# Stick-breaking attention scores: the keys' low part of two heads in one page, each head's product over 64 rows of the array

## The chip, the cores and the metric

The kernel runs on one core of one Trainium2 chip. The metric is device time in microseconds (us) of one execution. Before the change it is 1696.86 us, the median of three runs (1694.31 to 1698.92).

## The reference, cut to what matters

The layer normalises its input, runs three token mixers on it (stick-breaking attention, mLSTM, cross-attention), merges them and ends with a gated MLP. The change touches the scores of the first mixer, 8 heads of 64 dimensions over 1024 positions:

```
z = jnp.einsum('bhtd,bhsd->bhts', q[:, :, t0:t1], k[:, :, :t1]).astype(jnp.float32) * scale
strict = jnp.arange(t1)[None, :] < (t0 + q_pos)[:, None]
log_fail = jnp.where(strict, jax.nn.log_sigmoid(-z), 0.0)
log_after = lax.cumsum(log_fail, axis=3, reverse=True) - log_fail
w = jnp.where(strict, jnp.exp(jax.nn.log_sigmoid(z) + log_after), 0.0)
outs.append(jnp.einsum('bhts,bhsd->bhtd', w.astype(v.dtype), v[:, :, :t1]))
```

## The kernel before, in words

**Precision.** TensorE multiplies numbers of a reduced form (`fp32r` in the rows). For nearly fp32 results the kernel splits operands: hi is the rounded value, lo is the rest, and a product is hi·hi + hi·lo + lo·hi. The large projections write this as three matmuls of 512 columns (`mm3`, lines 149 to 151).

**Scores of two heads.** The heads are taken in four pairs p = 0 to 3. The projected queries of a pair fill 128 partitions, 64 per head. `sb_qk` (line 364) lays them out so that one matmul over 128 rows does two of the three products: page `qs[a]` of head a holds the query's hi in the head's own 64 partitions and its lo in the other 64; page `ks[a]` holds the key's hi in both halves. So `qs[a]·ks[a]` is hi·hi + lo·hi. The third product, the query's hi with the key's lo, uses a page `kz[a]` per head: the key's lo in the head's own 64 partitions and zeros in the other 64, written once per pair by two memsets of GpSimd (POOL).

**Pieces.** Scores are made in pieces: one block of 128 queries (`rb`) against up to 4 blocks of 128 keys, so a matmul has 128 to 512 columns. Each pair of heads has 12 pieces. For a piece `sb_weights` (line 404) issues for head 0 the 128-row product (line 410), on pieces with the diagonal block the mask (line 412), and the product with `kz` (line 413); then the same for head 1. The PSUM tile `z` has one bank per head, and there is a single such tile. ScalarE (ACT) makes two sigmoids of it (`f` and `g`, lines 415 and 416), VectorE (DVE) a running product and a multiply (422, 424).

**What stands around a piece.** The loop over pieces issues, in this order: the scores of piece n; on two pieces of three half a unit of the next pair's projection (lines 149 to 151; for p = 3 the mLSTM values); the weighted sum of an earlier piece (`sb_apply`, line 448, matmuls whose weights are 64 columns wide, head 0 to PSUM partitions 0 to 63 and head 1 to 64 to 127); the transposes of the piece before (`sb_turn`, line 434), copied out of PSUM by ACT (line 436, tile `y`). Line 448 waits for that copy. Each engine works its instructions in a fixed order, found by a scheduler at build time with priorities; pages come from a ring of 16 buffers (`pg`), so a page less shifts which buffer a later page gets.

Of the kernel before, what the change touches and what calls it, by code (L numbers as in the profile page):

```python
# [10 lines left out]
F32 = mybir.dt.float32  # L11
F32R = mybir.dt.float32r
# [26 lines left out]
T_SBQ, T_SBK, T_MLQ, T_MLK, T_MLO, T_XAQ, T_GATE = 0, 4, 8, 12, 16, 20, 24  # L39
# [3 lines left out]
def tile_hybrid_layer(ctx: ExitStack, tc: tile.TileContext, xT, memT, vecs, w_t, w_n, w_kv, w_if,  # L43
# [4 lines left out]
    nc = tc.nc  # L48
# [19 lines left out]
    def T(shape, tag, dt=F32, bufs=None):  # L68
        pool = {"mw": mlp, "mst": mlp, "ga": mlp, "gm": mlp,  "px": late[0]}.get(tag, sb)
        return pool.tile(shape, dt, tag=tag, name=nm(tag), bufs=bufs or BUFS[tag])  # L70

    def page(tag="pg", dt=F32):
        return T([P, S], tag, dt)
# [7 lines left out]
    def two(tag):  # L81
        return psx[0].tile([P, 2, HALF], F32, tag=tag, name=nm("ps_" + tag), bufs=1)
# [6 lines left out]
    def bank(tag):  # L89
        if tag in ("pj", "pv"):  # L90
            return ps.tile([P, HALF], F32, tag=tag, name=nm("ps_" + tag), bufs=2)
        if px1 is not None:
            if not spare.get(tag):
                t = two(tag)
                spare[tag] = [t[:, 1], t[:, 0]]
            return spare[tag].pop()
        return psx[0].tile([P, HALF], F32, tag=tag, name=nm("ps_" + tag), bufs=2)
# [4 lines left out]
    def hs(h):  # L102
        return slice(h * HALF, (h + 1) * HALF)

    def ts(t):
        return slice(t * P, (t + 1) * P)
# [32 lines left out]
    def wsplit(src, tag=None, eng=None, raw=None):  # L139
        if raw is None:  # L140
            raw = T([P, S], "raw")
            nc.sync.dma_start(raw, src)
        hi = T([P, S], tag or "whi", F32R)
        lo = T([P, S], tag or "wlo", F32R)
        split(raw, hi, lo, eng)
        return hi, lo

    def mm3(out, lh, ll, rh, rl, start, stop, more=False):
        nc.tensor.matmul(out, lh, rh, start=start, stop=False, skip_group_check=more)  # L149
        nc.tensor.matmul(out, lh, rl, start=False, stop=False, skip_group_check=more)  # L150
        nc.tensor.matmul(out, ll, rh, start=False, stop=stop, skip_group_check=more)  # L151
# [8 lines left out]
    def rstd(acc, n):  # L160

        nt = n // P
        pc = bank("tr")
        for t in range(nt):
            nc.tensor.matmul(pc[:, t:t + 1], acc[:, ts(t)], ones[:, :1], start=True, stop=True)
        return rstd_cols(pc[:, :nt], nt, D)
# [103 lines left out]
    def x_stats(xp):  # L270
        acc = []
        for i in range(4):
            sq = wide()
            nc.scalar.activation(sq, xp[i], AF.Square)
            acc.append(sq)
            if i:
                nc.vector.tensor_add(acc[0], acc[0], sq)
        a = acc[0][:, hs(0)]
        nc.vector.tensor_add(a, a, acc[0][:, hs(1)])
        return a  # L280
# [37 lines left out]
    r = rstd(x_stats(xp[1]), HALF)  # L318
# [16 lines left out]
    def proj_chunks(src, consume, halves=(1, 0)):  # L335

        with tc.high_priority(offset=SOON):
            wh, wl = wsplit(src)
        for h in halves:
            p = bank("pj")  # L340
            for k in range(KT):
                mm3(p, wh[:, ts(k)], wl[:, ts(k)], hh[k][:, hs(h)], hl[k][:, hs(h)], k == 0, k == KT - 1)
                if k == 3:
                    yield
            consume(h, p)
            yield
# [17 lines left out]
    def sb_qk(p):  # L364
        qs = [page(dt=F32R) for _ in range(2)]
        ks = [page(dt=F32R) for _ in range(2)]
        kz = [page(dt=F32R) for _ in range(2)]
        A, B = slice(0, 64), slice(64, 128)
        nc.gpsimd.memset(kz[0][B].bitcast(F32), 0.0)
        nc.gpsimd.memset(kz[1][A].bitcast(F32), 0.0)  # L370

        def eq(h, b):
            c = hs(h)
            nc.scalar.activation(qs[0][A, c], b[A], AF.Copy)
            nc.scalar.activation(qs[1][B, c], b[B], AF.Copy)
            nc.vector.tensor_sub(qs[0][B, c], b[A], qs[0][A, c].bitcast(F32))
            nc.vector.tensor_sub(qs[1][A, c], b[B], qs[1][B, c].bitcast(F32))

        def ek(h, b):
            c = hs(h)  # L380
            nc.scalar.activation(ks[0][A, c], b[A], AF.Copy)
            nc.scalar.activation(ks[1][B, c], b[B], AF.Copy)
            nc.scalar.activation(ks[0][B, c], b[A], AF.Copy)
            nc.scalar.activation(ks[1][A, c], b[B], AF.Copy)
            nc.vector.tensor_sub(kz[0][A, c], b[A], ks[0][A, c].bitcast(F32))
            nc.vector.tensor_sub(kz[1][B, c], b[B], ks[1][B, c].bitcast(F32))

        return (qs, ks, kz), lambda *a: itertools.chain(proj_chunks(w_t[T_SBQ + p], eq, *a),
                                                        proj_chunks(w_t[T_SBK + p], ek, *a))

    y_d = [dtile([4, P, S], f"y{b}_d") for b in range(3)]
# [10 lines left out]
    acc_pv = [None]  # L402

    def sb_weights(p, st, rb, o):
        qs, ks, kz = st
        w = min(4, NCH - rb - o) * P
        c = slice((rb + o) * P, (rb + o) * P + w)
        z = two("z")
        for a in range(2):
            nc.tensor.matmul(z[:, a, :w], qs[a][:, ts(rb)], ks[a][:, c], start=True, stop=False)  # L410
            if o == 0:
                nc.tensor.matmul(z[:, a, :P], ident_r, mask_r, start=False, stop=False, skip_group_check=True)
            nc.tensor.matmul(z[:, a, :w], qs[a][:, ts(rb)], kz[a][:, c], start=False, stop=True)
        f, g = T([P, 2, HALF + 1], "U"), T([P, 2, HALF], "U")
        nc.scalar.activation(f[:, :, 1:w + 1], z[:, :, :w], AF.Sigmoid, scale=-0.125)  # L415
        nc.scalar.activation(g[:, :, :w], z[:, :, :w], AF.Sigmoid, scale=0.125)
        if o == 0:
            nc.gpsimd.memset(f[:, :, 0:1], 1.0)
        else:
            nc.vector.tensor_copy(f[:, :, 0:1], carry[0])  # L420
        for a in range(2):
            nc.vector.tensor_tensor_scan(f[:, a, 1:w + 1], f[:, a, 1:w + 1], f[:, a, 1:w + 1],  # L422
                                         1.0 if o == 0 else f[:, a, 0:1], op0=ALU.mult, op1=ALU.bypass)
        nc.vector.tensor_mul(g[:, :, :w], g[:, :, :w], f[:, :, 0:w])
        carry[0] = f[:, :, w:w + 1]
        return g
# [31 lines left out]
    def gates_if():  # L458
        for h in (1, 0):
# [10 lines left out]
            yield  # L470

    st, chunks = sb_qk(0)
    early = []
    for b in range(2):
# [18 lines left out]
    a = x_stats(xp[0])  # L493
    for _ in range(1):
        next(vals)
    r = rstd(a, HALF)
# [115 lines left out]
    for p in range(4):  # L612
        now = st
        if p < 3:
            st, chunks = sb_qk(p + 1)
            chunks = chunks()
        else:
            chunks = nat_chunks(1, ev_v, [0, 1, 2, 3, 7, 6, 5, 4])
        for n, (rb, o) in enumerate(PIECES):
            g = sb_weights(p, now, rb, o)  # L620
            if n % 3 < 2:
                next(chunks, None)
            if (p, n) == (0, 2):
                next(rows_step)
            apply_next()
            turn_next()
            weights.append((p, rb, o, g))
        if p < 3:
            for _ in chunks:
                pass  # L630
# [401 lines left out]
    for i in range(3 * KT):  # L1032
        b, n = i // KT, i % KT
# [5 lines left out]
        for h in (1, 0):  # L1039
            p = bank("pj")  # L1040
            for j in range(4):
                c = slice(((n % 2) * 4 + j) * P, ((n % 2) * 4 + j + 1) * P)
# [362 lines left out]
```

## Time and profile before

| | |
|---|---|
| median of the runs shown | 1696.86 us |
| profiled execution | 1701.33 us |
| its span, first to last instruction | 1699.6 us |
| PE (TensorE matmul) busy | 1664.2 us, 98% |
| PEld (weight loads, beside PE) | 1337.9 us, 79% |
| DVE, ACT, POOL busy | 1196.2, 823.8, 71.5 us |
| score stage, about 115 to 327 us | 212 us of the span |

The busy times come from one profiled execution. A matmul's recorded duration is longer than the time until the next one can start, since matmuls are pipelined: the cost of one in a row of them is read from start to start. An idle time in square brackets is counted from the recorded end of the matmul before.

### The profile page before, as it was taken

The numbers are of one execution on the slowest core, as the hardware profiler recorded it, in microseconds if no ns is written. First come the engines' busy times: TensorE is split into PE (matmuls) and PEld (weight loads), VectorE is DVE, ScalarE is ACT, GpSimd is POOL, SyncE is SP. The second block draws the span as 40 slices with busy tenths as digits, with TensorE's granted clock in tenths as the row PEclk, the third lists the DMA queues.
The fourth block names the chain that finished last, engine by engine and source line by source line (L and its number), as shares of the span: only waits on it lengthen the run. The fifth ranks groups of instructions, "written<-read, shape, count | busy, mean of one in ns | idle before, by whom it ended". The sixth has DMA issues, their size and how long they took to land.

```text
span 1699.6 us, 21431 instructions
## 1 busy us (share of the span) xinstructions
PE 1664.2 (98%) x7927; PEld 1337.9 (79%) x7927; DVE 1196.2 (70%) x1752; ACT 823.8 (48%) x1293; POOL 71.5 (4%) x149
## 2 busy tenths in 40 slices
PE   8999999999999999999999999999999999999999
PEld 4777777787777887777788888688888888788887
DVE  5648777677944665555457747998877787789864
ACT  4547677545544444555412334465555555543531
POOL 1000000020000221100000000000000000000000
PEclk9999999999999999999999999999999999999999
DMA  8321011233324555432666255132232222486042
GB/s 295 143 64 32 26 39 50 95 119 129 113 99 138 164 182 170 152 99 98 236 194 197 86 194 199 44 130 75 79 105 77 75 75 75 152 330 235 25 143 75
DMA packets 99069, 212.73 MB, mean 125 GB/s; under 512 B 13184, under 2 KB 41088, under 8 KB 98964
## 3 DMA queue, kind: packets, MB, share of 16 engines
q1 hardware_dynamic: 98964, 211.35, 36.7%
q8 instruction: 63, 1.03, 0.3%
q14 instruction: 42, 0.34, 0.1%
HBM read 156.71 MB, written 54.61 MB: 124 GB/s over the span
## 4 chain that ended last, share of the span: by engine, by line
PE 86%; ACT 4%; DVE 4%; DMA 3%; issue 2%; SPq 1%; POOL 0%; POOLq 0%; ACTq 0%; DVEq 0%
PE ps_pj L149 14%; PE ps_pj L150 13%; PE ps_pj L151 13%; PE ps_pv L150 6%; PE ps_pv L151 6%; PE ps_pv L149 6%; PE ps_tr L149 4%; PE ps_tr L150 4%; PE ps_tr L151 4%; PE ps_z L151 2%; PE ps_z L150 2%; PE ps_z L149 2%; PE ps_pv L448 2%; PE ps_tr L434 2%; DMA y<-qk_d 1%
## 5 line engine op out<-in xcount | busy, mean ns | idle before, releaser
L150 PE MATMUL ps_pj<-h,whi 128*128 128x512 f32 x620 | 244.1, 394 | 0.0
L136 ACT ACTIVATE whi<-raw 128x512 fp32r<-128x512 f32 (+1 forms) x112 | 93.6, 835 | 185.4 <-PE ps_pj L150 82.9
L149 PE MATMUL ps_pj<-h,whi 128*128 128x512 f32 x412 | 163.6, 397 | 0.8 <-DVE U L1048 0.8
L149 PE MATMUL ps_pj<-pg,whi 128*128 128x512 f32 x396 | 155.3, 392 | 0.2 <-DVE pg L1046 0.2
L151 PE MATMUL ps_pj<-pg,wlo 128*128 128x512 f32 x380 | 148.1, 390 | 0.2 <-DVE wlo L137 0.2
L150 PEld LDWEIGHTS ps_pj<-h,whi 128*128 128x128 f32 x620 | 116.7, 188 | 24.7 <-issue 1.0
L151 PE MATMUL ps_pj<-h,wlo 128*128 128x512 f32 x332 | 131.4, 396 | 0.5 <-DVE wlo L137 0.4
L816 DVE SCALAR_TENSOR_TENSOR y<-U,vec,y 128x1023 f32<-128x1023 f32 x88 | 112.4, 1279 | 7.8 <-ACT y L814 7.8
L422 DVE TENSOR_TENSOR_SCAN U<-U 128x512 f32<-128x512 f32 (+3 forms) x96 | 88.6, 964 | 31.3 <-ACT U L415 30.4
L149 PEld LDWEIGHTS ps_pj<-h,whi 128*128 128x128 f32 x412 | 77.9, 189 | 16.6 <-DVE U L1048 1.2
L137 DVE TENSOR_TENSOR wlo<-raw,whi 128x1024 fp32r<-128x1024 f32 x54 | 66.0, 1222 | 33.7 <-ACT whi L136 33.6
L149 PEld LDWEIGHTS ps_pj<-pg,whi 128*128 128x128 f32 x396 | 74.4, 188 | 17.6 <-issue 1.6
L151 PEld LDWEIGHTS ps_pj<-pg,wlo 128*128 128x128 f32 x380 | 71.3, 188 | 15.7 <-DVE wlo L137 0.6
L136 ACT ACTIVATE whi<-pg 128x512 fp32r<-128x512 f32 (+1 forms) x59 | 43.4, 737 | 74.0 <-PE ps_pv L150 20.4
L150 PE MATMUL ps_pj<-pg,whi 128*128 128x512 f32 x188 | 74.9, 398 | 0.0
L151 PEld LDWEIGHTS ps_pj<-h,wlo 128*128 128x128 f32 x332 | 62.8, 189 | 14.8 <-DVE wlo L137 1.4
L150 PE MATMUL ps_pv<-h,whi 128*128 128x512 f32 x164 | 63.8, 389 | 0.0
L137 DVE TENSOR_TENSOR whi<-raw,whi 128x512 fp32r<-128x512 f32 x58 | 40.4, 697 | 32.6 <-ACT whi L136 32.6
L814 ACT ACTIVATE y<-U,vec 128x1024 f32<-128x1024 f32 x44 | 54.6, 1240 | 14.5 <-DVE U L720 14.4
L151 PE MATMUL ps_pj<-h,whi 128*128 128x512 f32 x156 | 61.5, 394 | 0.0
L436 ACT ACTIVATE y<-ps_tr 128x1024 f32<-128x1024 f32 (+3 forms) x48 | 39.0, 813 | 38.9 <-PE ps_tr L434 38.7
L151 PE MATMUL ps_tr<-pg,wlo 128*128 128x512 f32 x144 | 56.1, 389 | 0.0
(429 smaller groups left out, 4304.5 us busy)
## 6 DMA issues: line engine op xcount, KB each, us to landing
raw<-in_w_t_dram SPq DMA_DIRECT2D x29, 512.0 KB, 4.6
gate_d<-U SPq DMA_DIRECT2D x24, 512.0 KB, 3.1
U<-gate_d SPq DMA_DIRECT2D x24, 512.0 KB, 3.9
pg<-in_w_up_dram SPq DMA_DIRECT2D x22, 512.0 KB, 3.5
act_d<-y SPq DMA_DIRECT2D x22, 512.0 KB
pg<-in_w_t_dram SPq DMA_DIRECT2D x21, 512.0 KB, 3.7
raw<-in_w_dn_dram SPq DMA_DIRECT2D x18, 512.0 KB, 3.5
raw<-in_w_o_dram SPq DMA_DIRECT2D x16, 512.0 KB, 3.4
```

What stands on the lines that cost most here:

```text
L136: nc.scalar.activation(hi, src, AF.Copy)
L137: (eng or nc.vector).tensor_sub(lo, src, hi.bitcast(F32))
L149: nc.tensor.matmul(out, lh, rh, start=start, stop=False, skip_group_check=more)
L150: nc.tensor.matmul(out, lh, rl, start=False, stop=False, skip_group_check=more)
L151: nc.tensor.matmul(out, ll, rh, start=False, stop=stop, skip_group_check=more)
L422: nc.vector.tensor_tensor_scan(f[:, a, 1:w + 1], f[:, a, 1:w + 1], f[:, a, 1:w + 1], 1.0 if o == 0 else f[:, a, 0:1], op0=ALU.mult, op1=AL ...
L434: nc.tensor.transpose(pt[:, a, ts(j)], g[:, a, ts(j)], ident)
L436: nc.scalar.activation(wt[:, :, :w], pt[:, :, :w], AF.Copy)
L448: nc.tensor.matmul(pv[64 * a:64 * a + 64, ts(rb % 4)], sbv[s // 2][:, s % 2, (2 * p + a) * 64:(2 * p + a + 1) * 64], wt[:, a, ts(j)], star ...
L814: nc.scalar.activation(out, u, AF.Identity, bias=bias, scale=taps[0])
L816: nc.vector.scalar_tensor_tensor(out[:, :S - s], u[:, s:], taps[s], out[:, :S - s], op0=ALU.mult, op1=ALU.add)
```

## The change: what it does

The two pages `kz` become one page `kl`, with the key's lo of head 0 in partitions 0 to 63 and of head 1 in partitions 64 to 127; the memsets go. The third product of head a is now a matmul over the head's own 64 partitions alone, of `qs[a]` (its hi half) and `kl`. Both heads' third products stand together at the end of the piece, behind the four other matmuls (before, each stood behind its own head's). Numbers of matmuls, of columns, of ACT and DVE instructions stay as they are.

```
 def sb_qk(p):
...
-        kz = [page(dt=F32R) for _ in range(2)]
+        kl = page(dt=F32R)
         A, B = slice(0, 64), slice(64, 128)
-        nc.gpsimd.memset(kz[0][B].bitcast(F32), 0.0)
-        nc.gpsimd.memset(kz[1][A].bitcast(F32), 0.0)
...
-            nc.vector.tensor_sub(kz[0][A, c], b[A], ks[0][A, c].bitcast(F32))
-            nc.vector.tensor_sub(kz[1][B, c], b[B], ks[1][B, c].bitcast(F32))
+            nc.vector.tensor_sub(kl[A, c], b[A], ks[0][A, c].bitcast(F32))
+            nc.vector.tensor_sub(kl[B, c], b[B], ks[1][B, c].bitcast(F32))
...
 def sb_weights(p, st, rb, o):
...
         for a in range(2):
             nc.tensor.matmul(z[:, a, :w], qs[a][:, ts(rb)], ks[a][:, c], start=True, stop=False)
             if o == 0:
                 nc.tensor.matmul(z[:, a, :P], ident_r, mask_r, start=False, stop=False, skip_group_check=True)
-            nc.tensor.matmul(z[:, a, :w], qs[a][:, ts(rb)], kz[a][:, c], start=False, stop=True)
+        for a in range(2):
+            r = slice(64 * a, 64 * a + 64)
+            nc.tensor.matmul(z[:, a, :w], qs[a][r, ts(rb)], kl[r, c], start=False, stop=True)
```

On PE, this is one piece of the first pair of heads with 512 keys and the diagonal (`pg_272` and `pg_273` are the two `qs`, `pg_274` and `pg_275` the two `ks`, `pg_276` and `pg_277` the two `kz`, and in the changed kernel `pg_276` is `kl`). Before:

```order
L149 MATMUL ps_pj_1015<-h_102,whi_858 128x512
L410 MATMUL ps_z_1000<-pg_274,pg_272 128x512
L412 MATMUL ps_z_1000<-mask,ident 128x128
L413 MATMUL ps_z_1000<-pg_276,pg_272 128x512
L410 MATMUL ps_z_1000<-pg_275,pg_273 128x512
L412 MATMUL ps_z_1000<-mask,ident 128x128
L413 MATMUL ps_z_1000<-pg_277,pg_273 128x512
L150 MATMUL ps_pj_1015<-h_110,whi_858 128x512
```

The same place in PE's order of the changed kernel, whose lines 408, 410 and 413 are the product over 128 rows, the mask and the product over 64 rows:

```order
L149 MATMUL ps_pj_1009<-h_102,whi_852 128x512
L408 MATMUL ps_z_994<-pg_274,pg_272 128x512
L410 MATMUL ps_z_994<-mask,ident 128x128
L408 MATMUL ps_z_994<-pg_275,pg_273 128x512
L410 MATMUL ps_z_994<-mask,ident 128x128
L413 MATMUL ps_z_994<-pg_276,pg_272 128x512
L413 MATMUL ps_z_994<-pg_276,pg_273 128x512
L150 MATMUL ps_pj_1009<-h_110,whi_852 128x512
```

Head 0's third product moved behind head 1's first; what stands ahead of a piece and behind it is the same in all 48 pieces.

On ACT one instruction moves, at the passage from p = 2 to p = 3: the rounding of a block of value weights into a page (line 136, `pg` from `raw`). Before, it stands between the copy of a transposed piece and the sigmoids of the last piece of p = 2:

```order
L436 ACTIVATE y_2335<-ps_tr_2328 128x2x384 [waits PE_49,Activation_49]
L136 ACTIVATE pg_2396<-raw_2394 128x1024 [waits DMAHW4_49,PE_49]
L415 ACTIVATE U_2342<-ps_z_2337 128x2x512 [waits DVE_49,PE_49]
L416 ACTIVATE U_2343<-ps_z_2337 128x1024
L136 ACTIVATE pg_2402<-raw_2400 128x1024 [waits DMAHW6_49]
L436 ACTIVATE y_2365<-ps_tr_2356 128x1024 [waits PE_49,Activation_49]
```

In the changed kernel it stands twelve rows earlier on ACT, behind the sigmoids of another piece of p = 2:

```order
L415 ACTIVATE U_2211<-ps_z_2204 128x2x512 [waits PE_49,DVE_49,Activation_49,Pool_49]
L416 ACTIVATE U_2212<-ps_z_2204 128x1024
L136 ACTIVATE pg_2384<-raw_2382 128x1024 [waits DMAHW4_49]
L436 ACTIVATE y_2232<-ps_tr_2227 128x2x256 [waits PE_49,Activation_49]
L415 ACTIVATE U_2239<-ps_z_2234 128x2x384 [waits DVE_49,PE_49]
L416 ACTIVATE U_2240<-ps_z_2234 128x2x384
```

The page that it writes is free earlier, since four pages fewer have been taken from the ring; its wait for PE is gone, and the subtraction on DVE that belongs to it moves with it. All other instructions of ACT, DVE and SP keep their order, and POOL's lose the eight memsets.

## Rows read from the trace of the kernel before

**Rows 1.** The page, part 1: busy us (share of span) xinstructions.
```profile
span 1699.6 us, 21431 instructions
...
PE 1664.2 (98%) x7927; PEld 1337.9 (79%) x7927; DVE 1196.2 (70%) x1752; ACT 823.8 (48%) x1293; POOL 71.5 (4%) x149
```

**Rows 2.** Busy time by stretch, the four pairs of heads.
```profile
core 0: us, PE busy (x) PEld busy (x) DVE busy (x) ACT busy (x) POOL busy (x), PEclk, DMA share, GB/s
115.00:168.00 53.00, 50.16 (x338) 39.59 (x337) 46.27 (x84) 39.01 (x55) 2.45 (x8) 1.00 0.10 30
168.00:222.00 54.00, 52.99 (x383) 42.09 (x381) 42.09 (x51) 37.80 (x53) 2.66 (x10) 1.00 0.10 35
```

**Rows 3.** Instructions on tile `ps_z`: durations ns min/median/max, first and last start, forms.
```profile
L413 PE MATMUL ps_z<-pg,pg x96: 273/392/452, 115.3 to 326.1; 128*128 128x512 f32 x48, 128*128 128x128 f32 x16, 128*128 128x256 f32 x16, 128*128 128x384 f32 x16
```

**Rows 4.** Timeline of PE: start us, us, line, out<-in, weights (rows*columns), operand, count.
```profile
242.17 0.39 PE L150 MATMUL ps_pj<-h,whi 128*128 128x512 f32 x1
242.40 0.39 PE L151 MATMUL ps_pj<-h,wlo 128*128 128x512 f32 x1
242.72 0.88 PE L448 MATMUL ps_pv<-y,pg 128*64 128x128 f32 x12
...
244.37 0.30 PE L410 MATMUL ps_z<-pg,pg 128*128 128x128 f32 x1
...
244.85 0.45 PE L149 MATMUL ps_pj<-h,whi 128*128 128x512 f32 x1
245.84 1.09 PE L448 MATMUL ps_pv<-y,pg 128*64 128x128 f32 x16 [0.55 <-ACT y L436]
246.87 1.09 PE L434 MATMUL ps_tr<-ident,U 128*128 128x128 f32 x8
...
261.87 0.33 PE L413 MATMUL ps_z<-pg,pg 128*128 128x384 f32 x1
262.04 0.34 PE L410 MATMUL ps_z<-pg,pg 128*128 128x384 f32 x1
```

**Rows 5.** Timeline of PE around weights of 32 rows.
```profile
417.28 0.39 PE L151 MATMUL ps_pv<-pg,wlo 128*128 128x512 f32 x1
417.60 0.24 PE L586 MATMUL ps_tr<-ident,ga 32*128 32x32 f32 x1
...
419.61 0.50 PE L149 MATMUL ps_pv<-h,wlo 128*128 128x512 f32 x1 [1.64 <-ACT wlo L136]
419.94 0.40 PE L150 MATMUL ps_pv<-h,wlo 128*128 128x512 f32 x1
```

**Rows 6.** Timeline of PE: a piece with line 448 right behind it.
```profile
232.22 0.39 PE L413 MATMUL ps_z<-pg,pg 128*128 128x384 f32 x1
232.54 0.44 PE L448 MATMUL ps_pv<-y,pg 128*64 128x128 f32 x4
```

**Rows 7.** Who waited for whom, 115 to 327 us: us in total, times, longest.
```profile
PE ps_pv L448 <- ACT y L436: 4.1, 12, 0.5
PE ps_z L410 <- ACT U L416: 1.0, 1, 1.0
```

**Rows 8.** Timeline of PE: two more stops of line 448, and one at the next pair's start.
```profile
259.76 1.09 PE L448 MATMUL ps_pv<-y,pg 128*64 128x128 f32 x16 [0.30 <-ACT y L436]
...
274.00 0.88 PE L448 MATMUL ps_pv<-y,pg 128*64 128x128 f32 x12 [0.15 <-ACT y L436]
...
278.64 1.09 PE L448 MATMUL ps_pv<-y,pg 128*64 128x128 f32 x16 [0.23 <-ACT y L436]
280.00 1.06 PE L434 MATMUL ps_tr<-ident,U 128*128 128x128 f32 x8 [0.26 <-DVE U L424]
```

**Rows 9.** Timeline of ACT: the moved rounding (line 136), and idle time where it goes.
```profile
266.13 1.03 ACT L436 ACTIVATE y<-ps_tr 128x1024 f32<-128x1024 f32 x1 [2.02 <-PE ps_tr L434]
...
273.84 1.05 ACT L136 ACTIVATE pg<-raw 128x1024 fp32r<-128x1024 f32 x1
```

**Rows 10.** Instructions of line 369, a memset of POOL: durations ns, starts.
```profile
L369 POOL MEMSET pg<- x4: 947/952/953, 1.7 to 218.6; 64x1024 f32 x4
```

More of the change, by code (lines that the diff above doesn't have):

```diff
@@ L384, in ek @@
             nc.scalar.activation(ks[1][A, c], b[B], AF.Copy)
-            nc.vector.tensor_sub(kz[0][A, c], b[A], ks[0][A, c].bitcast(F32))
-            nc.vector.tensor_sub(kz[1][B, c], b[B], ks[1][B, c].bitcast(F32))
-        return (qs, ks, kz), lambda *a: itertools.chain(proj_chunks(w_t[T_SBQ + p], eq, *a),
+            nc.vector.tensor_sub(kl[A, c], b[A], ks[0][A, c].bitcast(F32))
+            nc.vector.tensor_sub(kl[B, c], b[B], ks[1][B, c].bitcast(F32))
+        return (qs, ks, kl), lambda *a: itertools.chain(proj_chunks(w_t[T_SBQ + p], eq, *a),
                                                         proj_chunks(w_t[T_SBK + p], ek, *a))
@@ L404, in sb_weights @@
     def sb_weights(p, st, rb, o):
-        qs, ks, kz = st
+        qs, ks, kl = st
         w = min(4, NCH - rb - o) * P
```

## The prediction, made before the changed kernel ran

> **What bounds the kernel now.** The page's first part shows PE busy 98% of the span, no other engine above 79% [rows 1]: what lengthens PE's work lengthens the time, and what shortens it helps only where PE does not then wait. The busy times by stretch show the same for the stage of the change, 115 to 327 us: a pair of heads takes 53 to 54 us, PE busy for 50 to 53 of them, ACT and DVE below 47, all at a granted clock of 1.00 [rows 2]. So I price the change on PE, from start to start in the timeline (recorded durations overlap), and then look in the list of waits for places where PE stops anyway.
>
> **The price of one matmul.** In a row of like matmuls one of 512 columns costs 0.23 us (242.17 to 242.40), one of 384 costs 0.17 (261.87 to 262.04), and four of 128 take 0.48 (244.37 to 244.85), 0.12 each [rows 4]. One of 256 lies between 0.12 and 0.17; I take 0.12. The third products (line 413) are 96, half of them 512 wide, 16 each of the other widths [rows 3]: 24 pieces have 512 columns, 8 each 384, 256 and 128.
>
> **What the change can save.** After it the two third products use different rows of the array and different PSUM banks. If they run side by side, each piece saves one matmul. No matmul of this trace does that with rows, but line 448 does with columns: its weights are 64 columns wide, its neighbours write different partitions, and 16 of them take 1.09 us, as long as 8 transposes over the whole array [rows 4]. I take it that row halves run in pairs too: saved are 24 x 0.23 + 8 x 0.17 + 16 x 0.12 = 8.8 us. The other end is nothing saved.
>
> **What it adds.** PE now goes from 128 rows to 64 and back in each of 48 pieces. Where the shape of the weights changes, the trace shows a gap: from line 151 to line 448 it is 0.32 us (242.40 to 242.72) instead of 0.23 [rows 4], and again 0.32 from line 151 to a matmul with 32 rows (417.28 to 417.60) [rows 5]. So 0.09 us go until the array is free. The weights have also not been loaded ahead then. What that costs shows where a whole-array matmul starts after idle time: its successor starts 0.33 us later (419.61 to 419.94) instead of 0.23, 0.10 more [rows 5]. A switch costs some 0.20 us, two per piece 0.40. Bounds: nothing for both, if 64 rows need no switch, and 0.51 for both, if the two heads' weights load one after the other (0.11 more, about the cost of a 128-column matmul). I take 0.40, since the two nearest kinds of partial weights both show the 0.09.
>
> The Trainium skill (TensorEngine Tiling (Array Packing), Key Properties) says that changing the tiling mode drains the engine, while a change of tile within a mode does not. That rule speaks against this change; the two gaps of 0.32 us agree with it for 64 columns and for 32 rows, and no run here shows it yet for 64 rows. By it the sum is the one below; without it, the first rival.
>
> **Piece by piece.** Two switches less one saved matmul: 512 columns 0.40 - 0.23 = +0.17 us, 384 columns +0.23, 256 and 128 columns +0.28. Over the stage 24 x 0.17 + 8 x 0.23 + 16 x 0.28 = 4.1 + 1.8 + 4.5 = +10.4 us.
>
> Three things come off it. (1) In five of the 48 pieces line 448 follows at once in PE's order, and there the second switch is paid already (0.32 us at 232.22 to 232.54) [rows 6]: -1.0 us. (2) PE stops for the tile `y` of line 448, 4.1 us in 12 places, and once 1.0 us for the sigmoids [rows 7]. `y` is copied by ACT from transposes that stand on PE ahead of the delayed piece, so a stop eats the piece's delay up to its own length. The stops of a pair of heads that have a piece just ahead are 0.55 us (a 128-column piece: eats 0.28) [rows 4], 0.30 and 0.15 us (512 columns: 0.17 and 0.15) [rows 8]. That is 0.6 us each for p = 0, 1, 2 and 0.28 for p = 3; the start of p = 0, where PE waits most, eats two more narrow pieces, 0.56. In sum -2.6 us. (3) The rounding of a weight block on ACT, 1.05 us, leaves its place ahead of the last sigmoids of p = 2 and goes where ACT has 2.02 us idle behind it [rows 9]. The two stops at the start of p = 3, 0.23 and 0.26 us [rows 8], go with it: -0.5 us; nothing, if the next copy is late instead.
>
> The rest is hidden. The memsets of POOL (0.95 us each [rows 10]) stand on an engine that is busy 4% [rows 1]; the matmuls' wait for them goes, and no PE stop is put down to them. DVE and ACT write as many elements as before, at the same partitions. The four pages that are not taken make buffers free earlier, so transfers can only start earlier; later stages are in the same order. No wait is added. Behind the last third product stand ACT's sigmoids, which start later by the same 0.17 to 0.28 us, and PE's next work, which the sum holds already.
>
> **Sum.** 10.4 - 1.0 - 2.6 - 0.5 = +6.3 us. On the profiled execution (span 1699.6, 1701.33 with what lies around it) that makes 1707.6; it is 4.5 above the median of the runs, in which the same work is done, so I put the 6.3 on the median 1696.86: 1703 us.
>
> **Rivals.**
> 1. *Sixty-four rows cost no switch, and the pair runs side by side.* Then 8.8 us of matmuls go; in the three pieces of a pair that stand ahead of a stop the gain is waited away (0.12 + 0.23 + 0.23 us, four times: 2.3), and the 0.5 of ACT comes on top: -7.0 us, 1690. For it: the pairs of line 448, which need no gap between the two halves [rows 4]. Against it: both kinds of partial weights in the trace begin with 0.32 us [rows 4, 5]. The Trainium skill (TensorE: Matmul & The Clock Gate, The mechanism, in Part 3) has the weights for other rows pulled ahead of running matmuls and such matmuls starting about 4 ns apart; read alone, it gives this rival.
> 2. *Switches are paid and nothing runs side by side.* This is the slower case at its worst: 48 x 0.40 = 19.2, less 1.0 for the five pieces, less some 4 at the stops (they are full then), less 0.5: +13.7, 1710.5. It decides as soon as the second half starts 0.12 to 0.23 us behind the first. For it: the trace shows no pair of row halves. Against it: line 448.
> 3. *Side by side, but the weights load in turn.* 48 x 0.11 = 5.2 more than my sum, some 0.8 of it eaten by stops: +10.7, 1707.6. For it: weight loads fill the time of narrow matmuls. Against it: 128-row and 64-column loads already overlap with matmuls in the stream.
> 4. *The change does not do what it says: 64 rows are worked like 128, no pair, no switch.* Only the 0.5 us remains: 1696.4. Against it: the 32-row gap.
>
> **Chances.** My forecast 0.56, with a range of its own of +3 to +9 us (a switch at 0.16 or 0.24 us shifts the sum by about 3, after the stops); rival 1: 0.12; rival 2: 0.09; rival 3: 0.13; rival 4: 0.10. What a measurement of this kernel can tell from no change is 0.3%, 5.1 us. The forecast lies 1.2 above that border, so 0.6 of its chance is slower and 0.4 the same: slower 0.34 + 0.09 + 0.12 = 0.55, same 0.22 + 0.01 + 0.10 = 0.33, faster 0.12. The range 1693 to 1710 leaves out most of rivals 1 and 2 and holds the rest.
>
> **What would show it.** In the profile after: the two matmuls of line 413 with 64 rows start within some 10 ns of each other; ahead of them 0.32 us instead of 0.23, behind them about 0.42 until the next whole-array matmul, whose successor comes 0.33 us later. The z part of a piece with 512 columns grows by 0.17 us, one with 128 by 0.28; the four stretches of 53 us grow by 1 to 2 us each, the stops of line 448 shrink, and the stages behind the scores are only shifted. Wrong it is, if the pair starts 0.1 us apart or more (rivals 2, 3), if no gap stands ahead of it (1, 4), or if the stage's growth stays in it while a later stage gives it back.

## The result, and the profile after

The changed kernel takes 1703.49 us (median of 7 runs, 1701.37 to 1706.5) against 1697.66 us before (7 runs): a ratio of 1.0038, 95% interval 1.0027 to 1.0049, that is 5.8 us slower by the medians (4.6 to 8.3 by the interval). The prediction was 1703.0, slower, by two switches of the array's shape per piece that cost more than one saved matmul. The mechanism was right. One term of the sum, the saved matmul, was priced too low, which made the stage's growth too large, and part of the measured time is not the stage's.

The page's first part of the changed kernel; the span was 1699.6 us before [rows 1]:

```profile
span 1704.6 us, 21415 instructions
...
PE 1671.0 (98%) x7927; PEld 1332.4 (78%) x7927; DVE 1195.4 (70%) x1752; ACT 823.1 (48%) x1293; POOL 63.6 (4%) x141
```

PE's busy time grew by 6.8 us with the same number of matmuls; POOL's fell by the memsets. Where the growth lies is told by the instructions on tile `ps_z` (durations in ns, first and last start in us). Before, the products over 128 rows:

```profile
L410 PE MATMUL ps_z<-pg,pg x96: 221/392/484, 115.1 to 325.8; 128*128 128x512 f32 x48, 128*128 128x128 f32 x16, 128*128 128x256 f32 x16, 128*128 128x384 f32 x16
```

The same product after, and the third product, which answers to rows 3:

```profile
L408 PE MATMUL ps_z<-pg,pg x96: 221/398/484, 116.2 to 331.1; 128*128 128x512 f32 x48, 128*128 128x128 f32 x16, 128*128 128x256 f32 x16, 128*128 128x384 f32 x16
L413 PE MATMUL ps_z<-pg,pg x96: 323/466/502, 116.7 to 331.4; 64*128 64x512 f32 x48, 64*128 64x128 f32 x16, 64*128 64x256 f32 x16, 64*128 64x384 f32 x16
```

The first piece starts 1.1 us later (116.21 instead of 115.12), the last one 5.5 us later (330.76 instead of 325.29): from the first piece to the last the stage grew by 4.4 us. The 1.1 us come from ahead of it: 0.33 us at a wait at 50 us, 0.35 among the first matmuls, and 0.45 at the very first, which starts at 6.75 us instead of 6.30, when its data have landed:

```profile
6.75 5.82 PE L226 MATMUL ps_z<-raw,pg 128*128 128x512 f32 x7 [6.75 <-DMA raw<-in_w_kv_dram]
```

In the ten profiles below the first matmul starts between 6.34 and 6.97 us, without relation to what was changed; I count it as scatter of one execution.

Now one piece of 512 columns without a mask in the changed kernel, on PE's timeline (columns as in rows 4):

```profile
276.30 0.71 PE L408 MATMUL ps_z<-pg,pg 128*128 128x512 f32 x2
276.95 0.50 PE L413 MATMUL ps_z<-pg,pg 64*128 64x512 f32 x2
277.38 0.50 PE L149 MATMUL ps_pj<-whi,h 128*128 128x512 f32 x1
277.72 0.39 PE L150 MATMUL ps_pj<-wlo,h 128*128 128x512 f32 x1
277.95 0.40 PE L151 MATMUL ps_pj<-whi,h 128*128 128x512 f32 x1
```

The two third products are one row: both within 0.50 us, as long as a single one lasts, so they run side by side (their starts are 3 to 4 ns apart in every pair). From the pair to the next matmul it is 0.43 us (276.95 to 277.38), and that one's successor comes 0.34 us later instead of 0.23. These are the figures forecast (0.42 and 0.33). Ahead of the pair it is 0.33 us (276.62, the second matmul of line 408, to 276.95), where 0.32 was forecast. The weight loads of the same stretch show that nothing is loaded ahead over a switch:

```profile
276.94 0.19 PEld L413 LDWEIGHTS ps_z<-pg,pg 64*128 64x128 f32 x2 [0.37 <-issue]
277.38 0.19 PEld L149 LDWEIGHTS ps_pj<-whi,h 128*128 128x128 f32 x1 [0.24 <-issue]
277.48 0.19 PEld L150 LDWEIGHTS ps_pj<-wlo,h 128*128 128x128 f32 x1
```

The loads of the pair and of the matmul behind it begin with their own matmuls, at 276.94 and 277.38 us; the load of line 150 begins at 277.48, 0.24 us ahead of its matmul.

The waits of PE in 112 to 333 us, which answer to rows 7:

```profile
PE ps_pv L448 <- ACT y L436: 2.1, 8, 0.4
PE ps_z L408 <- ACT U L416: 0.8, 1, 0.8
```

The stops for `y` shrank from 4.1 to 2.1 us, as they should where they eat a piece's delay. At the start of p = 3 the two stops of rows 8 are gone; counted from start to start they give back 0.31 and 0.33 us, 0.64 in sum. Line 136 now stands in what was idle time of ACT:

```profile
265.83 1.07 ACT L136 ACTIVATE pg<-raw 128x1024 fp32r<-128x1024 f32 x1
...
270.76 1.02 ACT L436 ACTIVATE y<-ps_tr 128x1024 f32<-128x1024 f32 x1 [1.96 <-PE ps_tr L434]
```

One statement made ahead of the prediction is wrong: what stands ahead of a piece is not the same in all 48. The first piece of p = 3 stands four matmuls of the projection earlier in PE's order. Before, it followed lines 151, 149, 150 and 151:

```profile
276.44 0.39 PE L151 MATMUL ps_pj<-whi,h 128*128 128x512 f32 x1
276.77 0.33 PE L410 MATMUL ps_z<-pg,pg 128*128 128x128 f32 x1
```

In the changed kernel it follows the transposes, and the four come behind it:

```profile
279.75 0.93 PE L434 MATMUL ps_tr<-ident,U 128*128 128x128 f32 x7
280.61 0.33 PE L408 MATMUL ps_z<-pg,pg 128*128 128x128 f32 x1
...
281.46 0.50 PE L151 MATMUL ps_pj<-whi,h 128*128 128x512 f32 x1
```

So this piece's start moves forward without a gain for the stage: it comes 3.83 us later than before, the last piece of p = 2 4.78, the second one of p = 3 4.32.

### The profile page after: what moved, and what is told of

The parts are those of the page before. It is cut to its first block, busy times and chain, and to the rows that moved or that the text cites. A ratio compares the mean times of both kernels' runs of the same rounds, so it can differ in the third digit from the quotient of the medians.

```text
span 1704.6 us, 21415 instructions
## 1 busy us (share of the span) xinstructions
PE 1671.0 (98%) x7927; PEld 1332.4 (78%) x7927; DVE 1195.4 (70%) x1752; ACT 823.1 (48%) x1293; POOL 63.6 (4%) x141
## 4 chain that ended last, share of the span: by engine, by line
PE 86%; DVE 4%; DMA 4%; ACT 3%; issue 1%; SPq 1%; POOL 0%; POOLq 0%; ACTq 0%; DVEq 0%
PE ps_pj L149 14%; PE ps_pj L150 13%; PE ps_pj L151 13%; PE ps_pv L150 6%; PE ps_pv L151 6%; PE ps_pv L149 6%; PE ps_tr L149 4%; PE ps_tr L151 4%; PE ps_tr L150 4%; PE ps_z L151 2%; PE ps_z L150 2%; PE ps_z L149 2%; PE ps_pv L448 2%; PE ps_tr L434 2%; DMA y<-qk_d 1%
## 5 line engine op out<-in xcount | busy, mean ns | idle before, releaser
L137 DVE TENSOR_TENSOR wlo<-raw,wlo 128x512 fp32r<-128x512 f32 x58 | 39.9, 688 | 24.4 <-ACT wlo L136 24.1
```

The source lines that it names most:

```text
L137: (eng or nc.vector).tensor_sub(lo, src, hi.bitcast(F32))
```

## The experiments

**1. The order alone** (base: the kernel before).

```
             nc.tensor.matmul(z[:, a, :w], qs[a][:, ts(rb)], ks[a][:, c], start=True, stop=False)
...
+        for a in range(2):
             nc.tensor.matmul(z[:, a, :w], qs[a][:, ts(rb)], kz[a][:, c], start=False, stop=True)
```

> The kernel before with one thing of the change: both heads' third products (128 rows, with the zero rows) stand together at the end of the piece. Theory (the time goes into switching the array between 128 and 64 rows): as before, 1697.7 us, within 1 us, since the matmuls and their weight loads are the same in number and size. Rival (the order costs it: the masks and the last products stand otherwise, the sigmoids start otherwise): some 1703, as the changed kernel.

Measured: 1697.61 us against 1697.50, ratio 1.0004 (0.9995 to 1.0013). The place of the two products costs nothing.

**2. The changed kernel with 128 rows** (base: the changed kernel, as in 3 and 4). This is the whole change but for the shape of the 96 matmuls.

```
-            r = slice(64 * a, 64 * a + 64)
-            nc.tensor.matmul(z[:, a, :w], qs[a][r, ts(rb)], kl[r, c], start=False, stop=True)
+            nc.tensor.matmul(z[:, a, :w], qs[a][:, ts(rb)], kl[:, c], start=False, stop=True)
```

> The changed kernel with its third products over all 128 rows instead of 64 (no zero rows, so the products of the other head's rows get into the scores: the output is another). Pages, order of all engines and POOL's work are those of the changed kernel; only the shape of 96 matmuls differs. Theory: the switches and the pairing go together, 1697 us: the level of before less about 1.0 us for the rounding on ACT that moved out of the passage to p = 3. Rival (the cost is in the pages, the order or the earlier start of transfers): 1702 to 1704.

Measured: 1697.37 us, ratio 0.9997 (0.9988 to 1.0006). So the 64 rows are all of the loss; the pages and the order cost nothing, the moved first piece of p = 3 included, which stands in this kernel as in the changed one. The 1.0 us that I expected from the rounding on ACT is 0.63 us in the trace at that passage, and too little for the times.

**3. Each half by itself.**

```
-        for a in range(2):
             r = slice(64 * a, 64 * a + 64)
             nc.tensor.matmul(z[:, a, :w], qs[a][r, ts(rb)], kl[r, c], start=False, stop=True)
```

> The changed kernel with the third products over 64 rows, but each right behind its own head's products, as the kernel before has them. Theory (each change of rows costs about 0.20 us, 0.06 less behind a mask): four switches per piece and no pair, 32 x 0.68 + 16 x 0.80 = 34.6 us, less 1 for the pieces followed by line 448, some 4 eaten by stops and 1 on ACT: 1726. Rival A (64 rows need no switch, the loss lies in the pair): 1697. Rival B (only the unhidden weight load costs, no drain: 0.1 us per switch): 1711.

Measured: 1723.53 us against 1697.50, ratio 1.0157 (1.0143 to 1.0171): +26.0 us where 28.6 were expected and the rivals said 0 and 14. A piece of 512 columns on PE's timeline of this kernel (line 412 is the third product):

```profile
230.41 0.47 PE L408 MATMUL ps_z<-pg,pg 128*128 128x512 f32 x1
230.81 0.50 PE L412 MATMUL ps_z<-pg,pg 64*128 64x512 f32 x1
231.24 0.50 PE L408 MATMUL ps_z<-pg,pg 128*128 128x512 f32 x1
231.67 0.50 PE L412 MATMUL ps_z<-pg,pg 64*128 64x512 f32 x1
232.10 0.50 PE L149 MATMUL ps_pj<-h,whi 128*128 128x512 f32 x1
```

Every matmul between two switches takes 0.43 us from start to start, in either direction, instead of 0.23: a switch costs 0.20 us. I read it as the drain (the array runs empty before its shape changes) and the load that isn't hidden, together.

**4. Both products over the same 64 rows.**

```
-            r = slice(64 * a, 64 * a + 64)
+            r = slice(0, 64)
```

> The changed kernel with both third products over the same 64 rows (head 1's takes head 0's rows, so its scores are others). Two switches per piece remain, the pair can't run side by side. Theory: the second product costs its full time again, 24 x 0.23 + 8 x 0.17 + 16 x 0.12 = 8.8 us, less some 1 at the stops: 1711. Rival A (the pairing saves nothing in the changed kernel): 1703.5, as the changed kernel. Rival B (weights for rows in use are not loaded ahead at all): another 0.1 to 0.2 us per piece, 1716 to 1721.

Measured: 1708.68 us, ratio 1.0063 (1.0049 to 1.0077): 11.2 us more than before (1697.50) and 5.2 more than the changed kernel. A piece of 512 columns without a mask:

```profile
279.55 0.71 PE L408 MATMUL ps_z<-pg,pg 128*128 128x512 f32 x2
280.19 0.73 PE L413 MATMUL ps_z<-pg,pg 64*128 64x512 f32 x2
280.85 0.50 PE L149 MATMUL ps_pj<-whi,h 128*128 128x512 f32 x1
```

From the pair's start to the next matmul it is 0.66 us instead of 0.43: the pairing is worth 0.23 us here, a whole matmul, as priced. Of the 8.8 us over all pieces the stage shows 5.8 (it grew by 10.1 us against before, the changed kernel by 4.4 on the same count); the stops for `y` fell once more, to 1.0 us in 4 places. I had given the stops 1 us of the 8.8; they and the other waits took 3. Rivals A and B fall.

**5. Line 448 right behind the scores** (base: the kernel before; then the same edit on the changed kernel).

```
             g = sb_weights(p, now, rb, o)
+            apply_next()
+            turn_next()
+            weights.append((p, rb, o, g))
             if n % 3 < 2:
                 next(chunks, None)
             if (p, n) == (0, 2):
                 next(rows_step)
-            apply_next()
-            turn_next()
-            weights.append((p, rb, o, g))
```

> The kernel before with another order of the loop over pieces: the weighted sum (line 448) and the transposes come right behind a piece's scores, the next projection's half unit behind them. On PE line 448 then follows a piece directly in 44 of 48 pieces. Switches between whole-array weights and 64-column weights are as many as before. Theory: about as before, 1697.5 us, within 2 us (stops for the tile y move). Rival (the stops grow, since less work stands between the copy of y and its use): 1700 or more.

> The changed kernel with the same new order of the loop: behind the pair over 64 rows line 448 comes directly in 46 of 48 pieces (5 before), so the way back to the whole array is paid once for both. Theory: 41 switches of 0.20 us less, 8.2 us, of which some 2 are handed back at stops that ate them: 1697.5 us, within 2 us of the kernel before in the same order. Rival (what costs is the way into 64 rows, or the pair itself): no more than 2 us less than the changed kernel, 1702 or more.

Measured: 1708.61 and 1712.02 us, against 1697.27 before (ratios 1.0069, 1.0056 to 1.0083, and 1.0088, 1.0074 to 1.0102). The theory fell on the base: the new order itself costs 11 us. PE's transposes now come too early and wait for DVE, for its multiply (line 424) and for the copy that carries the running product on (line 420); the waits of the first of the two kernels:

```profile
PE ps_tr L434 <- DVE U L424: 6.6, 8, 1.3
PE ps_z L410 <- ACT U L416: 3.4, 7, 1.0
PE ps_tr L434 <- DVE U L420: 2.4, 4, 0.7
```

The difference of the two is 3.4 us instead of 5.8 in the old order, and I had expected none. In the traces it is none up to the first piece of p = 3: from the stage's first piece to there both take 172.5 us, within 0.02. The pieces are as priced, too: in the changed kernel those of 512 columns with the mask are 0.09 us shorter, but for four that end at a stop, and those without it 0.02, where one switch less the saved matmul gives 0.20 - 0.28 = -0.08 and 0.20 - 0.23 = -0.03 (on the 0.28, see the next part). So the traces bear out that the way back is paid once. Behind that point, where PE's order differs as well, a stop of 1.34 us for DVE appears in the second kernel, and behind the stop the granted clock is 0.50, the lower level of 1.2 GHz; eight transposes take 1.94 us instead of 1.09:

```profile
291.71 1.94 PE L434 MATMUL ps_tr<-ident,U 128*128 128x128 f32 x8 [1.34 <-DVE U L424]
```

```profile
core 0: us, PE busy (x) PEld busy (x) DVE busy (x) ACT busy (x) POOL busy (x), PEclk, DMA share, GB/s
292.00:294.00 2.00, 2.00 (x10) 1.90 (x9) 1.78 (x4) 0.25 (x1) 0.10 (x1) 0.50 0.17 39
```

The four runs of this kernel all have a mean granted clock of 0.997, the five of the other 0.998 to 1.000. A line through the 62 runs of the kernel before that stand beside experiments 1, 5, 7 and 8 gives 1.6 us for each 0.001 of it; by that, an estimate, some 3 of the 3.4 us go with the lower clock. The times alone don't tell the theory from the rival (1702 or more).

**6. Pairs only where they should pay** (base: the first kernel of 5, with its zero rows).

```
-            nc.tensor.matmul(z[:, a, :w], qs[a][:, ts(rb)], kz[a][:, c], start=False, stop=True)
+            if o or w < 3 * P:
+                nc.tensor.matmul(z[:, a, :w], qs[a][:, ts(rb)], kz[a][:, c], start=False, stop=True)
+        if o == 0 and w >= 3 * P:
+            for a in range(2):
+                r = slice(64 * a, 64 * a + 64)
+                nc.tensor.matmul(z[:, a, :w], qs[a][r, ts(rb)], kz[a][r, c], start=False, stop=True)
```

> The kernel before in the new order of the loop, with its two pages and zeros, where only the pieces of 384 and 512 columns with the mask (24 of 48) take their third products over 64 rows, together and ahead of line 448; the others keep 128 rows. Theory: each such piece saves a matmul of 0.23 us and the 0.06 behind a mask for one switch of 0.19: -0.10 us on 20 pieces of 512, -0.04 on 4 of 384, some 2 us less than the kernel before in the new order, 1695.5. Rival (every partial shape costs more than a pair saves): 1698 to 1702.

Measured: 1709.73 us, ratio 1.0071 (1.0059 to 1.0084), beside 1708.61 for its base, where 2 us less were expected. In the trace 16 of the 20 pieces of 512 columns are 0.09 us shorter, near the 0.10 expected; the other four end at a stop that eats it, and the stage is 0.7 us shorter than the base's. The times can't tell the two apart: a gain in the time isn't shown, and it is no version to use.

**7. Without masks, before and after.**

```
-            if o == 0:
-                nc.tensor.matmul(z[:, a, :P], ident_r, mask_r, start=False, stop=False, skip_group_check=True)
```

> The kernel before without the 64 mask matmuls (scores on and above the diagonal are left in). It is the base for the next one. Each mask matmul costs some 0.11 us: 64 x 0.11 = 7 us less, some handed back at stops: about 1691.

> The changed kernel without the mask matmuls. In the changed kernel a piece of 512 columns with the mask grew by 0.11 us and one without by 0.17. Theory: a mask matmul of 128 columns is shorter than the weight load behind it, which shows before the change as 0.06 us at the next matmul; the switch's drain hides that. Then without masks all pieces of 512 columns grow by 0.17 and those of 256 and 128 by 0.27 against the previous kernel, and the stage by about 6 us instead of 4.4. Rival (the smaller growth comes from elsewhere, as the first piece's place): the pieces that had masks still grow by 0.11, the stage by 4.4.

Measured: 1691.33 us (0.9967, 0.9954 to 0.9979) and 1697.23 us (1.0005, 0.9996 to 1.0015). Piece by piece the 20 pieces of 512 columns that had a mask now grow by 0.17 us at the median (0.11 with the mask), those of 256 by 0.27 (0.21); the stage grows by 7.0 us instead of 4.4. A piece of 512 in the second kernel (line 411 is the third product):

```profile
245.69 0.72 PE L408 MATMUL ps_z<-pg,pg 128*128 128x512 f32 x2
246.34 0.50 PE L411 MATMUL ps_z<-pg,pg 64*128 64x512 f32 x2
246.77 0.50 PE L150 MATMUL ps_pj<-h,whi 128*128 128x512 f32 x1
247.11 0.40 PE L151 MATMUL ps_pj<-h,wlo 128*128 128x512 f32 x1
```

So the mask matmul is what made the growth of the masked pieces smaller. Those of 128 columns missed the expectation: 0.18 us, as with the mask. There the third product itself is narrow, and the kernel before shows the load behind it, masks or not (0.28 us from 277.50 to 277.78 instead of 0.23; the rows are of the kernel before, with its masks):

```profile
277.38 0.28 PE L413 MATMUL ps_z<-pg,pg 128*128 128x128 f32 x1
277.50 0.45 PE L149 MATMUL ps_pj<-whi,h 128*128 128x512 f32 x1
277.78 0.40 PE L150 MATMUL ps_pj<-wlo,h 128*128 128x512 f32 x1
```

The two medians differ by 5.9 us, no more than with the masks (5.8): a stage longer by 2.7 us in the traces is within what the intervals of the times leave open.

**8. The masks off TensorE** (base: the kernel before, without its mask matmuls).

```
         if o == 0:
+            for t, v in ((f[:, :, 1:P + 1], 1.0), (g[:, :, :P], 0.0)):
+                nc.gpsimd.affine_select(out=t, in_=t, pattern=[[0, 2], [1, P]], compare_op=ALU.is_gt, fill=v,
+                                        base=0, channel_multiplier=-1)
             nc.gpsimd.memset(f[:, :, 0:1], 1.0)
```

> The kernel before (third products over 128 rows with zero rows) with its masks moved off TensorE: no mask matmul; instead POOL overwrites, behind ACT's sigmoids, the masked part of f with 1 and of g with 0, two instructions of 128x256 elements (0.41 us each for that shape in the profile before) on 32 pieces. Theory (PE bounds the stage, POOL is idle there): the 5.6 us that leaving the masks out gave come, less 1 to 2 us for the 0.8 us that stand between the sigmoids and DVE's scan where PE waits for that chain: 1692 to 1693.5. Rival (the longer chain sets the stage): 1697 or more.

Measured: 1694.98 us against 1697.18, ratio 0.9984 (0.9974 to 0.9994): 2.2 us faster than before and 8.5 less than the changed kernel's median, the fastest version with the whole computation here. It gives 2.2 of the 5.6 us that leaving the masks out gave. POOL's instruction took 0.74 us on average (0.41 to 1.44) instead of the 0.41 I had taken, and PE's transposes wait 4.8 us for DVE, which now starts behind POOL, where they waited 1.7 us without masks (experiment 7, the first kernel):

```profile
L417 POOL TENSOR_SCALAR_AFFINE_SELECT U<-U 128x256 f32<-128x256 f32 x64 | 47.4, 744 | 131.5 <-ACT U L413 122.1 <-ACT U L414 9.0
```

```profile
PE ps_tr L435 <- DVE U L425: 2.6, 4, 1.1
PE ps_pv L449 <- ACT y L437: 2.4, 6, 0.6
PE ps_tr L435 <- DVE U L421: 2.2, 4, 0.6
```

## Why the prediction was right, and where its sum was off

**The switch.** Right in both parts and in both directions: 0.43 us instead of 0.23 for a matmul between two switches (experiment 3). The Trainium skill (TensorEngine Tiling (Array Packing), Key Properties) has a change of the tiling mode drain the engine; for 64 rows the trace now agrees, with 0.10 us more than in a row ahead of the pair. Another 0.11 goes to the load that begins only with the matmul. Rivals 1 and 4 fall with this.

**The pair.** Right: side by side, worth a whole matmul (experiment 4). The Trainium skill (TensorE: Matmul & The Clock Gate, The mechanism, in Part 3) gives 4 ns between the starts; the trace has 3 to 4. Rivals 2 and 3 fall.

**The pieces.** Growth of one piece, from its first matmul to the second one behind it, in us:

| piece | count | forecast | measured, median |
|---|---|---|---|
| 512 columns, no mask | 3 | 0.17 | 0.17 |
| 512, mask | 19 | 0.17 | 0.11 |
| 384, no mask | 4 | 0.23 | 0.22 |
| 256, no mask / mask | 4 / 4 | 0.28 | 0.28 / 0.21 |
| 128, mask | 4 | 0.28 | 0.18 |
| 128, no mask (ahead of a stop) | 4 | 0.00 | 0.00 |
| line 448 behind it | 5 | -0.03 to 0.03 | -0.03 to 0.00 |

The sum over all pieces, with a 384-column piece at the start of p = 0 that a stop ate whole, is 6.1 us; forecast were 8.3 on the same count (10.4 less 1.0, less the 1.1 that the narrow pieces lose at once). Nearly all of the difference lies in the pieces with a mask or with 128 columns. This is the mis-sized term: I priced the saved matmul at its time in a row of like matmuls, 0.23 us for 512 columns and 0.12 for 128. Behind a mask a third product of 512 columns took 0.28 us, as this piece of the kernel before shows (266.73 to 267.02):

```profile
266.68 0.22 PE L412 MATMUL ps_z<-mask,ident 128*128 128x128 f32 x1
266.73 0.44 PE L413 MATMUL ps_z<-pg,pg 128*128 128x512 f32 x1
267.02 0.39 PE L149 MATMUL ps_pj<-h,whi 128*128 128x512 f32 x1
```

From the mask's start to the next matmul's it is 0.06 us. The weight load for that next matmul starts with the mask, and the load after it 0.11 us later (266.68 and 266.79 us). I read it that the matmul behind a mask still waits for its weights and is done 0.06 us late. The same piece in the changed kernel:

```profile
271.08 0.22 PE L410 MATMUL ps_z<-mask,ident 128*128 128x128 f32 x1
271.23 0.50 PE L413 MATMUL ps_z<-pg,pg 64*128 64x512 f32 x2
271.66 0.50 PE L149 MATMUL ps_pj<-h,whi 128*128 128x512 f32 x1
```

From the pair to the next matmul it is 0.43 us here too (271.23 to 271.66). So before the change the 0.06 us falls behind each of the 64 masks, after it only behind head 0's 32; behind head 1's the switch covers it. Experiment 7 shows it for the masks.

**The stops and ACT.** From 6.1 to the stage's 4.4 us (from start to start of the first and the last piece) there are 0.64 us at the start of p = 3, forecast 0.5, and some 1.1 at stops beyond the narrow pieces, forecast 1.5. The kinds were right, and the sizes differ by 0.1 and 0.4 us, in opposite directions.

**What stays open.** The stage explains 4.4 us in the profiles, the times say 5.8 (4.6 to 8.3). The rest of the profiled span, +0.7, lies ahead of the stage (+1.1) and behind it (-0.4). The changed kernel is also 6.1 us above its twin with 128 rows (experiment 2), whose stage is 5.1 us shorter in the trace. Whether the last microsecond is scatter or an effect that one profile doesn't show, these runs don't settle. So the hit of the total, within 0.5 us, is in part luck: the stage was forecast 1.9 us too long (6.3 against 4.4), and what the times show beyond the stage was not forecast.

## What to carry to other kernels

Count switches of the array's shape before packing small matmuls: each cost 0.20 us here, nearly one 512-column matmul, so a single pair per switch in and out loses. By these prices several pairs in a row would pay; no run here has them. With a neighbour that switches anyway behind the pair, the pieces of 512 columns got shorter by up to 0.09 us (experiments 5 and 6), but no time shows a gain. Zero rows cost a 128-row matmul nothing: with other numbers in their place it is 1697.37 us against 1697.50 (experiment 2). Look for narrow matmuls on the bound engine: here the masks cost about as much as the whole change (5.6 and 5.8 us), and an idle engine took them over for a gain of 2.2 us. Before reading where a piece starts, compare PE's order there: the first piece of p = 3 started earlier because it had been moved.

## What the runs showed of the hardware that I had not expected

A mask matmul of 128 columns costs the same 0.11 us among matmuls of 512 columns as 128-column matmuls do in a row, but only half of it shows at its own place (266.68 to 266.73 us before the change): the other half falls on the matmul behind it, and a switch at that place hides it. The mean granted clock differs from run to run by some 0.001, and with it the time: of the runs of the kernel before counted in experiment 5, the 25 with 0.999 have a median of 1695.8 us, the 30 with 0.998 one of 1698.0. POOL's masking of 128x256 elements took 0.74 us on average in this stage (0.41 to 1.44) and 0.43 us for the same shape at another place of the same kernel; the reason was not looked for.
